# Turning q and k of a transformer's second layer by VectorE blocks and GpSimd copies instead of TensorE transposes

## The chip, the cores and the metric

The kernel runs on one core of a Trainium2 chip. The metric is the device time of one execution in microseconds. A core has five engines that run side by side, each with its own queue of instructions worked off in order: TensorE (PE in the profile; the loads of its weights are PEld), VectorE (DVE), ScalarE (ACT), GpSimd (POOL) and SyncE (SP), which issues the DMAs here. Engines wait for each other by semaphores.

## The reference

An encoder of two layers on 256 tokens of 2048 features, all in float32. Each layer has a mixer sub-layer and a gated MLP. What matters here is the mixer's beginning:

```python
h = rmsnorm(x, norm_mix[l]) * (1.0 + sc_a) + sh_a
qa, ka, va, qb, kb, vb, ga, gb = split_cols(h @ w_in[l])
qa = rotary_partial(rmsnorm(qa.reshape(B, S, HA, HEAD_DIM), qn_a[l]), pos)
ka = rotary_partial(rmsnorm(ka.reshape(B, S, GA, HEAD_DIM), kn_a[l]), pos)
ya = window_attention(qa, ka, va, sink_a[l]) @ w_proj_a[l]
qb = rmsnorm(qb.reshape(B, S, HB, HEAD_DIM), qn_b[l])
kb = rmsnorm(kb.reshape(B, S, HB, HEAD_DIM), kn_b[l])
yb = neighbourhood_attention(qb, kb, vb, rel_bias_b[l]) @ w_proj_b[l]
merged = jax.nn.sigmoid(ga) * ya + jax.nn.sigmoid(gb) * yb
```

Mixer A has 8 query heads on 2 key heads, mixer B 8 heads; a head has 128 features. q and k are normalised for each head and token, scaled by a gain per feature, and in mixer A rotated in the first 32 features. Both attentions are softmaxes over the 256 tokens with a mask (A, with a sink logit) or a bias (B).

## The kernel before, in words

The weights (units of 128 x 2048 numbers, `ws`) come from HBM one after the other in the order of their use. Each unit is split into two halves by `unit_steps`: ScalarE casts a half to a rounded part (L319), VectorE subtracts it from the weights to get the rest (L320), both into a tile `hl` with four buffers. TensorE multiplies with three matmuls for each product (rounded by rounded, rounded by rest, rest by rounded: L336 to L338 in `feature_block`, L399 to L401 in `tokens`).

The projection to q, k and v is done in nine groups of 512 columns, group 0 to 8. Group 0 holds the keys and values of mixer A, 1 and 2 its queries (four heads each); 3, 4, 5 hold keys, values and queries of mixer B's first four heads, 6, 7, 8 those of the others. A group is four units long. `tokens` leaves a group with the 256 tokens on partitions, in two PSUM tiles `ps_t` of 128 tokens. The attention wants q and k with the features on partitions, so each group but the values' is turned in `qk_rows`:

- at once: squares summed per head by ScalarE (L569), roots by VectorE and GpSimd (`rsqrt`, L462 and L463);
- `norm`: VectorE multiplies by the roots into `qn` (L578), a tile with one buffer, and in groups 0 to 2 rotates (L593 to L595);
- `turn`: TensorE transposes each head's 128x128 block of `qn` into PSUM (L602), and ScalarE scales by the gain into the pack of the mixer (L603). Then the group counts as ready.

The background work hangs on `bg`, whose `tick` runs at the end of each unit. `defer` puts a function at the next tick: `norm` runs three ticks after the group, `turn` four. A job such as `attention` is stepped at a rate, a number of steps per tick. In each step of `attention` every living head goes one stage on, and one more head starts if the group that it waits for is ready. The stages of a head (`head_a`, `head_b`, `attend`) are: splitting of q and k; scores and softmax; turning of the probabilities; their split and the split of v; the product with v (`po`). In the second layer the probabilities are already turned without TensorE, by `turned_blocks`: VectorE transposes all 32x32 blocks (L293), and GpSimd puts the blocks in their places with 16 copies (L298).

The functions only trace instructions. The order on each engine is made afterwards by a planner (Tile's scheduler), which takes from the instructions that it expects to be ready the one that was traced first. So an instruction traced late can stand early in its engine's queue.

In the second layer the stretch runs thus: 8 units of mixer A's gate, the nine groups (36 units), the remaining gate (8), the projection of mixer A (8), mixer B's gate (16). All A heads must be done before the projection of mixer A, all B heads before that of mixer B.

## Time and profile before

| what | value |
|---|---|
| median of 3 runs | 2657.92 us (2656.72 to 2659.6) |
| profiled execution | 2660.64 us, its span 2658.7 us |
| TensorE busy | 2646.4 us of the span |
| VectorE busy | 2116.5 us |
| ScalarE busy | 1407.9 us |
| GpSimd busy | 194.0 us |
| GpSimd's copies L298 in the second layer | 256, from 1511.0 to 1748.6 us |
| transposes L602 of q and k | 104, 52 of them in the second layer |

Rows of the profile name a line of the kernel, an engine, an operation, the tile written and those read, and the shapes (partitions x elements). A row of the timeline begins with its start in the span and its duration; in square brackets stands how long the engine had been idle before it, and what ended that. In a row of groups, the numbers behind the bar are busy us, mean ns of one, and the idle time before. A row for a tile or a line gives the shortest, the median and the longest duration in ns, and the first and the last start. "PE sc L629 <- ACT packB L603" in the waits is a wait of TensorE, at the instruction that writes `sc`, for ScalarE's that writes `packB`; total us, times and the longest follow. A cast or a matmul's record can overlap the next one on its engine.

### The profile page before, as it was taken

Reading aid. Unit: us, or ns where it says so; the run is one execution under the profiler, and the core shown is the slowest. Engines: PE = TensorE matmul, PEld = TensorE weight load, DVE = VectorE, ACT = ScalarE, POOL = GpSimd, SP = SyncE. Lnnn points to the kernel's source line nnn. Section 1 sums busy time; section 2 is a strip of 40 time slices with the busy share of each in tenths; the row PEclk is TensorE's granted clock in tenths of the full one; section 3 lists DMA queues with packets and bytes.
Section 4 is the critical chain, followed back from the end, with each engine's and each line's share of the span. In section 5 each row is a group of like instructions: output and inputs, shape, how many; then the busy total and the mean of one; then the engine's idle time right before and its main releaser. Section 6 shows DMA issues by size and latency. Waiting matters only on the chain.

```text
span 2658.7 us, 51010 instructions
## 1 busy us (share of the span) xinstructions
PE 2646.4 (100%) x21192; PEld 2561.3 (96%) x21192; DVE 2116.5 (80%) x2975; ACT 1407.9 (53%) x2284; POOL 194.0 (7%) x281
## 2 busy tenths in 40 slices
PE   9999999999999999999999999999999999999999
PEld 7888899999999999999998889999999999999999
DVE  8898998897987888788886677868888866655664
ACT  5445865456653555355554566645565445544553
POOL 0001100000000000000000177610000000000000
PEclk9999999999999999999999999999999999999999
DMA  9988779885778788877856666766747775555554
GB/s 359 350 329 300 257 296 353 319 327 193 283 294 297 282 293 296 297 288 285 296 213 255 237 236 235 255 256 260 279 180 286 295 254 191 191 197 193 196 190 143
DMA packets 102042, 700.43 MB, mean 263 GB/s; under 512 B 12721, under 2 KB 15025, under 8 KB 17969
## 3 DMA queue, kind: packets, MB, share of 16 engines
q1 hardware_dynamic: 101810, 697.17, 71.3%
q8 instruction: 166, 2.72, 0.4%
q14 instruction: 66, 0.54, 0.1%
HBM read 695.03 MB, written 2.10 MB: 262 GB/s over the span
## 4 chain that ended last, share of the span: by engine, by line
PE 88%; DVE 5%; POOL 2%; ACT 2%; DMA 1%; issue 1%; DVEq 0%; ACTq 0%; POOLq 0%
PE ps L336 26%; PE ps L338 26%; PE ps L337 26%; PE ps_t L401 3%; PE ps_t L400 3%; PE ps_t L399 3%; POOL p L298 2%; DVE hl L320 2%; DMA aw<-in_aw 1%; DVE aw L230 1%; ACT hl L319 1%; PE sc L629 1%; PE po L667 1%; POOL qrs L463 0%; ACT qsq L569 0%
## 5 line engine op out<-in xcount | busy, mean ns | idle before, releaser
L320 DVE TENSOR_TENSOR hl<-w,hl 128x1024 fp32r<-128x1024 f32 x928 | 1129.8, 1224 | 308.6 <-ACT hl L319 304.6
L319 ACT CAST hl<-w 128x1024 fp32r<-128x1024 f32 x928 | 969.7, 1048 | 704.7 <-PE ps L338 494.0
L336 PE MATMUL ps<-h,hl 128*128 128x256 f32 x3328 | 922.5, 277 | 1.3 <-DVE ya L948 0.6
L337 PE MATMUL ps<-h,hl 128*128 128x256 f32 x3328 | 919.7, 276 | 0.0
L338 PE MATMUL ps<-h,hl 128*128 128x256 f32 x3328 | 919.6, 277 | 0.0
L336 PEld LDWEIGHTS ps<-h,hl 128*128 128x128 f32 x3328 | 624.8, 188 | 2.3 <-DVE ya L948 0.8
L337 PEld LDWEIGHTS ps<-h,hl 128*128 128x128 f32 x3328 | 625.2, 188 | 0.4 <-DVE h L492 0.2
L338 PEld LDWEIGHTS ps<-h,hl 128*128 128x128 f32 x3328 | 624.3, 188 | 0.0
L230 DVE CUSTOM_DVE_ANT_0 aw<-aw,cact,ab 128x2048 f32<-128x2048 f32 x189 | 443.8, 2349 | 73.8 <-DMA aw<-in_aw 73.4
L399 PE MATMUL ps_t<-hl,h 128*128 128x512 f32 x576 | 223.4, 393 | 2.1 <-ACT h L491 1.6
L400 PE MATMUL ps_t<-hl,h 128*128 128x512 f32 x576 | 224.9, 391 | 0.4
L401 PE MATMUL ps_t<-hl,h 128*128 128x512 f32 x576 | 224.3, 390 | 0.0
L1027 DVE SCALAR_TENSOR_TENSOR u<-ps,cw,u 128x255 f32<-128x255 f32 x304 | 146.1, 481 | 63.0 <-ACT u L1025 58.9
L1025 ACT ACTIVATE u<-ps,cw 128x256 f32<-128x256 f32 x152 | 85.7, 564 | 157.0 <-PE ps L338 156.9
L336 PE MATMUL ps<-merged,hl 128*128 128x256 f32 x512 | 141.8, 278 | 0.8 <-DVE m L425 0.8
L338 PE MATMUL ps<-merged,hl 128*128 128x256 f32 x512 | 141.7, 277 | 0.0
L337 PE MATMUL ps<-merged,hl 128*128 128x256 f32 x512 | 141.7, 277 | 0.0
L337 PE MATMUL ps<-act_o,hl 128*128 128x256 f32 x512 | 141.4, 276 | 0.0
L338 PE MATMUL ps<-act_o,hl 128*128 128x256 f32 x512 | 141.4, 276 | 0.0
L336 PE MATMUL ps<-act_o,hl 128*128 128x256 f32 x512 | 141.2, 276 | 0.0
L399 PEld LDWEIGHTS ps_t<-hl,h 128*128 128x128 f32 x576 | 107.9, 188 | 25.4 <-ACT h L491 2.6
L400 PEld LDWEIGHTS ps_t<-hl,h 128*128 128x128 f32 x576 | 108.1, 188 | 24.0 <-DVE hl L320 2.1
(239 smaller groups left out, 4774.5 us busy)
## 6 DMA issues: line engine op xcount, KB each, us to landing
w<-in_ws SPq DMA_DIRECT2D x463, 1024.0 KB, 4.9
aw<-in_aw SPq DMA_DIRECT2D x189, 1024.0 KB, 6.1
p<-in_bias SPq DMA_DIRECT2D x16, 256.0 KB, 4.5
x<-in_xT SPq DMA_DIRECT2D x4, 512.0 KB, 5.4
aw_o<-in_aw SPq DMA_DIRECT2D x2, 1024.0 KB, 12.5
out<-x SPq DMA_DIRECT2D x16, 128.0 KB, 2.2
w<-in_ws SPq DMA_DIRECT2D x2, 512.0 KB, 11.8
aw_b<-in_aw SPq DMA_DIRECT2D x1, 1024.0 KB, 17.1
```

Of the source, the lines that this page charges most:

```text
L230: nc.vector.tensor_tensor_reduce(out=raw[:], in0=raw[:], in1=cact[:], scale=1.0, scalar=ab[:, i : i + 1], op0=ALU.mult, op1=ALU.add, accum ...
L298: nc.gpsimd.tensor_copy(out=dst[a : a + BLOCK, :, :, b : b + BLOCK], in_=blocks[b : b + BLOCK, :, :, a : a + BLOCK])
L319: nc.scalar.copy(hl[:, 0], r)
L320: nc.vector.tensor_tensor(out=hl[:, 1], in0=r, in1=hl[:, 0].bitcast(F32), op=ALU.subtract)
L336: nc.tensor.matmul(out, hi, act[0], start=first, stop=False)
L337: nc.tensor.matmul(ps[:, :S], hi, act[1], start=False, stop=False)
L338: nc.tensor.matmul(out, lo, act[0], start=False, stop=last)
L399: nc.tensor.matmul(ps[:], xh, hi, start=kc == kcs[0], stop=False)
L400: nc.tensor.matmul(ps[:], xh, lo, start=False, stop=False)
L401: nc.tensor.matmul(ps[:], xl, hi, start=False, stop=kc == kcs[-1])
L1025: nc.scalar.activation(out=u, in_=ps, func=AF.Identity, scale=w[:, 1:2], bias=w[:, 3:4])
L1027: nc.vector.scalar_tensor_tensor(out=u[:, to], in0=ps[:, of], scalar=w[:, j : j + 1], in1=u[:, to], op0=ALU.mult, op1=ALU.add)
```

## The change

In the second layer, groups 0, 1, 2 and 8 are no longer transposed by TensorE. VectorE transposes the 32x32 blocks of `qn` in place, GpSimd puts them into the pack with 16 copies (of 32 partitions and 128 elements in group 0, 256 in the others), and three ticks later ScalarE scales the pack in place by the gain; then the group is ready. `qn` is laid out without holes for that. The first layer and groups 3, 5 and 6 keep the transposes.

In the second layer the `attention` job is added after group 1 instead of group 2, at 0.4 steps a tick instead of 0.43. The first four A heads wait for groups 0 and 1, the other four for group 2; before, all waited for group 2.

```diff
-ATT = [1.288, 0.43]
+ATT = [1.288, 0.4]
+EARLY = {1: 2}
+MOVED_QK = [(), (0,1,2,8)]
+QK_STEPS = 3
...
+    def moved_blocks(dst, src):
+
+        for b in range(0, P, BLOCK):
+            for a in range(0, P, BLOCK):
+                nc.gpsimd.tensor_copy(
+                    out=dst[a : a + BLOCK, :, :, b : b + BLOCK], in_=src[b : b + BLOCK, :, :, a : a + BLOCK]
+                )
+
...
-            qn = at.tile([P, 2, 4, HEAD], F32, name="qn", tag="qn", bufs=1)
+            qn = at.tile([P, 8 * HEAD], F32, name="qn", tag="qn", bufs=1)[:, : 2 * n]
+            qn = qn.rearrange("p (t h d) -> p t h d", t=2, d=HEAD)
...
         def turn(qn):
+            if moved:
+                nc.vector.transpose(out=qn, in_=qn)
+                moved_blocks(dst.rearrange("p h (t s) -> p h t s", t=2), qn.rearrange("p t h d -> p h t d"))
+
+                def scaled():
+                    nc.scalar.activation(out=dst, in_=dst, func=AF.Identity, scale=gain)
+                    then()
+
+                later(QK_STEPS, scaled)
+                return
...
-            todo = [(3, head_a, i) for i in range(HA)] + [(6 + 3 * (i // 4), head_b, i) for i in range(HB)]
+            todo = [(EARLY[l] + i // 4, head_a, i) if l in EARLY else (3, head_a, i) for i in range(HA)] + [(6 + 3 * (i // 4), head_b, i) for i in range(HB)]
...
-                if g == 2:
+                if g == (1 if l in EARLY else 2):
                     bg.add(job, ATT[l])
```

The calls of `qk_rows` pass `g in MOVED_QK[l]` as `moved`; `turned_blocks` calls `moved_blocks` for its copies.

More of the change, by code (lines that the diff above doesn't have):

```diff
@@ L295, in turned_blocks @@
         dst = src.rearrange("p t (n k) -> p (t n k)", n=n).rearrange("p (n t k) -> p n t k", n=n, t=2)
-        for b in range(0, P, BLOCK):
-            for a in range(0, P, BLOCK):
-                nc.gpsimd.tensor_copy(
-                    out=dst[a : a + BLOCK, :, :, b : b + BLOCK], in_=blocks[b : b + BLOCK, :, :, a : a + BLOCK]
-                )
+        moved_blocks(dst, blocks)
     def unit_steps(l, u, by_halves=False):
@@ L559, in level, with qk_rows @@
             return z, sh
-    def qk_rows(pss, heads, rot, gain, dst, then):
+    def qk_rows(pss, heads, rot, gain, dst, then, moved=False):
         cols = 0
@@ L575, in norm @@
         def norm():
-            qn = at.tile([P, 2, 4, HEAD], F32, name="qn", tag="qn", bufs=1)
+            qn = at.tile([P, 8 * HEAD], F32, name="qn", tag="qn", bufs=1)[:, : 2 * n]
+            qn = qn.rearrange("p (t h d) -> p t h d", t=2, d=HEAD)
             for t, ps in enumerate(pss):
                 nc.vector.tensor_tensor(
-                    out=qn[:, t, :heads],
+                    out=qn[:, t],
                     in0=ps[:, cols : cols + n].rearrange("p (h d) -> p h d", d=HEAD),
@@ L584, in norm @@
             if rot is not None:
-                x1, x2 = qn[:, :, :heads, :HALF], qn[:, :, :heads, HALF:ROT]
+                x1, x2 = qn[:, :, :, :HALF], qn[:, :, :, HALF:ROT]
                 tab = [rot[:, i].unsqueeze(2).broadcast_to([P, 2, heads, HALF]) for i in range(4)]
@@ L930, in encoder @@
                 if g == 0:
-                    qk_rows(pss, GA, rots[1], gains[:, 1:2], kTa, turned)
+                    qk_rows(pss, GA, rots[1], gains[:, 1:2], kTa, turned, g in MOVED_QK[l])
                 elif g < 3:
-                    qk_rows(pss, 4, rots[0], gains[:, 0:1], dst, turned)
+                    qk_rows(pss, 4, rots[0], gains[:, 0:1], dst, turned, g in MOVED_QK[l])
                 elif vcol is None:
-                    qk_rows(pss, 4, None, gains[:, 3:4] if g in (3, 6) else gains[:, 2:3], dst, turned)
+                    qk_rows(pss, 4, None, gains[:, 3:4] if g in (3, 6) else gains[:, 2:3], dst, turned, g in MOVED_QK[l])
                 else:
                     turned()
-                if g == 2:
+                if g == (1 if l in EARLY else 2):
                     bg.add(job, ATT[l])
```

## Prediction

> **What bounds the kernel now.** First the page's busy line and its chain of waits, then the stretches of the second layer that the change touches, then the waits of PE in them.

> ```profile
> span 2658.7 us, 51010 instructions
> ...
> PE 2646.4 (100%) x21192; PEld 2561.3 (96%) x21192; DVE 2116.5 (80%) x2975; ACT 1407.9 (53%) x2284; POOL 194.0 (7%) x281
> ...
> PE 88%; DVE 5%; POOL 2%; ACT 2%; DMA 1%; issue 1%; DVEq 0%; ACTq 0%; POOLq 0%
> ```

> ```profile
> core 0: us, PE busy (x) PEld busy (x) DVE busy (x) ACT busy (x) POOL busy (x), PEclk, DMA share, GB/s
> 1421.00:1510.00 89.00, 89.00 (x406) 73.83 (x406) 60.31 (x86) 48.75 (x101) 6.00 (x4) 1.00 0.66 242
> 1510.00:1602.00 92.00, 92.00 (x447) 77.43 (x446) 69.49 (x115) 58.92 (x132) 61.38 (x100) 1.00 0.61 225
> 1602.00:1669.00 67.00, 66.56 (x560) 65.45 (x559) 54.25 (x89) 44.17 (x95) 44.01 (x68) 1.00 0.70 252
> ```

> ```profile
> PE sc L629 <- ACT packB L603: 0.4, 1, 0.4
> ```

> TensorE is the bound: busy for all but 12.3 us of a span of 2658.7, at clock 1.00, and over the whole stretch from 1377 to 1850 us it waited once, for 0.4 us (last fence), for the evacuation of group 8's transposes. VectorE has a fifth to a third of these stretches free, ScalarE a third to a half. GpSimd does almost nothing until 1510, and then works two thirds of the time on the heads' copies. So the change can gain only what it takes off TensorE, and can lose only by making TensorE wait. It waits when the split weights (hl) come late, since ScalarE (L319) and VectorE (L320) make them in order behind everything else that stands in their queues.

> **What is removed from TensorE.** Groups 1, 2 and 8 lose 8 transposes each, group 0 (two heads) 4: 28 of the second layer's 52. The record of one lasts 0.272 us, but PE's records overlap; what counts is from start to start.

> ```profile
> L602 PE MATMUL qtp<-ident,qn 128*128 128x128 f32 x52 | 6.8, 272 | 0.0
> ```

> ```profile
> 1463.53 0.39 PE L400 MATMUL ps_t<-hl,h 128*128 128x512 f32 x1
> 1463.76 0.39 PE L401 MATMUL ps_t<-hl,h 128*128 128x512 f32 x1
> 1463.99 1.03 PE L602 MATMUL qtp<-ident,qn 128*128 128x128 f32 x8
> 1464.78 0.48 PE L399 MATMUL ps_t<-hl,h 128*128 128x512 f32 x1
> 1465.09 0.39 PE L400 MATMUL ps_t<-hl,h 128*128 128x512 f32 x1
> ```

> ```profile
> 1441.71 0.60 PE L602 MATMUL qtp<-ident,qn 128*128 128x128 f32 x4
> 1442.07 0.48 PE L399 MATMUL ps_t<-hl,h 128*128 128x512 f32 x1
> 1442.38 0.39 PE L400 MATMUL ps_t<-hl,h 128*128 128x512 f32 x1
> ```

> Matmuls of 512 columns start 0.23 us apart. From the first transpose of eight to the second matmul behind them it is 1465.09 - 1463.99 = 1.10 us; less the 0.23 of the matmul between, eight cost 0.87 us. Four cost 1442.38 - 1441.71 - 0.23 = 0.44. Together 3 x 0.87 + 0.44 = 3.05 us, and with the 0.4 us wait of sc for group 8's evacuation, which goes too, **3.5 us**. The excess of start distances elsewhere in the stretch does not hang on the transposes.

> [...]

> **What is added beside TensorE.** The rows that price it: a block transpose, an evacuation, a cast of 1024 elements.

> ```profile
> L293 DVE STREAM_TRANSPOSE packB<-p x8: 700/712/712, 1633.2 to 1738.6; 128x512 f32<-128x512 f32 x8
> ```

> ```profile
> L603 ACT ACTIVATE packB<-qtp,gains 128x512 f32<-128x512 f32 x8 | 5.0, 682 | 0.5 <-PE qtp L602 0.5
> ```

> ```profile
> L319 ACT CAST hl<-w 128x1024 fp32r<-128x1024 f32 x928 | 969.7, 1048 | 704.7 <-PE ps L338 494.0
> ```

> VectorE: one block transpose for each group, in place. A 128x512 one takes 0.71 us, so 0.71 for group 0 and between 0.71 and 1.42 for each of the others; I take 1.4, 4.9 us in all. They fit in the free time of the stretches above (28.7 of 89 us, 12.8 of 67). ScalarE: two evacuations of 0.68 us become one instruction over 1024 elements, priced by the hl cast of that size, 1.05: a small gain off the path, priced at nothing. The changed layout of qn and the reads of the rotary on it have the same counts and sizes: nothing.

> ```profile
> L298 POOL COPY p<-spare x16: 285/290/2316, 1511.0 to 1518.9; 32x128 f32<-32x128 f32 x16
> ```

> ```profile
> masks.py:197 POOL MEMSET ident<- 128x128 f32 x1 | 0.2, 205 | 0.3 <-POOLq L1174 0.3
> ...
> L1174 POOL MEMSET const-float32-0.0<- 128x1 f32 x1 | 0.1, 99 | 0.2 <-issue 0.2
> ```

> GpSimd: 64 copies. Group 0's are 32x128, like the 256 of the heads; the others have 32x256, which no row shows. Below they can't be under the 0.285 us of 32x128, above not over twice that, 0.57. Nearest are the fills: 127 more elements cost 205 - 99 = 106 ns. So I take 0.39, or 1.6 us more for 16 copies.

> **The wait that is added.** The scaling on ScalarE now follows 16 copies. QK_STEPS sets it three ticks later in the program (a tick is a unit of weights, 24 of the matmuls above, 5.5 us). But that is only its priority. The norm of group 8 stands three ticks, 16 us, behind its squares and roots, and ran right behind the roots:

> ```profile
> 1614.36 1.64 POOL L463 TENSOR_TENSOR qrs<-qss,mhalf 128x8 f32<-128x8 f32 x1 [1.72 <-DVE qss L462]
> ```

> ```profile
> 1616.03 0.69 DVE L578 TENSOR_TENSOR qn<-ps_t,qrs 128x512 f32<-128x512 f32 x1 [1.81 <-POOL qrs L463]
> ```

> So an instruction is queued where the planned order has its inputs ready. Queued behind it on ScalarE are the hl casts, and behind those VectorE's subtractions and TensorE. The trace shows this very wait once, at head 0 of mixer A:

> ```profile
> 1511.04 8.18 POOL L298 COPY p<-spare 32x128 f32<-32x128 f32 x16 [15.99 <-DVE spare L293]
> ```

> ```profile
> 1512.38 1.06 ACT L319 CAST hl<-w 128x1024 fp32r<-128x1024 f32 x1
> 1519.25 0.62 ACT L411 CAST pT<-p 128x512 fp32r<-128x512 f32 x1 [5.80 <-POOL p L298]
> 1519.77 3.89 ACT L319 CAST hl<-w 128x1024 fp32r<-128x1024 f32 x4
> ```

> ```profile
> 1512.17 2.35 DVE L230 CUSTOM_DVE_ANT_0 aw<-aw,cact,ab 128x2048 f32<-128x2048 f32 x1 [1.26 <-DMA aw<-in_aw]
> ...
> 1520.85 1.23 DVE L320 TENSOR_TENSOR hl<-w,hl 128x1024 fp32r<-128x1024 f32 x1 [5.10 <-ACT hl L319]
> ```

> ```profile
> 1522.64 0.40 PE L399 MATMUL ps_t<-hl,h 128*128 128x512 f32 x1
> ```

> Sixteen copies took 8.18 us; ScalarE came to its cast 2.4 us after they began (1519.25 - 5.80 - 1511.04) and stood 5.8 us. The half unit cast behind it was ready at 1520.85 + 1.23 = 1522.08, and TensorE took it up at 1522.64 without idling: 0.6 us were left. So a wait of ScalarE for GpSimd is free up to about **6.4 us**, and costs TensorE one for one beyond.

> The copies' time holds waits of their own: the longest of these sixteen lasted 2.316 us, beside the 2.35 us of L230. [...]

> How far sixteen copies of a head stretch:

> ```profile
> 1620.41 12.36 POOL L298 COPY p<-packA 32x128 f32<-32x128 f32 x16 [4.41 <-DVE packA L293]
> 1633.96 7.71 POOL L298 COPY p<-packB 32x128 f32<-32x128 f32 x16 [1.18 <-DVE packB L293]
> 1645.41 12.63 POOL L298 COPY p<-packB 32x128 f32<-32x128 f32 x16 [3.74 <-issue]
> ```

> *Group 0*: the case of head 0, 5.8 us, nothing lost. If its copies stretch to 12.63, as in the last row, the wait is 10.2 and 3.8 are lost.

> *Groups 1 and 2*: 8.18 + 1.6 = 9.8 us of copies. ScalarE comes to the scaling 2.4 us behind their begin if the order expects no more of the larger copies, and at 2.4 x 9.8 / 8.18 = 2.9, or up to 3.1 by the bare copies, if it does. I take 3.1: a wait of 6.7, 0.3 lost by each. Ends: nothing (copies as short as 32x128), and with 0.57 us each 12.6 of copies, a wait of 10.2 and 3.8 lost by each.

> *Group 8* comes when GpSimd is occupied (the first two rows of the last fence):

> ```profile
> 1617.84 0.69 DVE L578 TENSOR_TENSOR qn<-ps_t,qrs 128x512 f32<-128x512 f32 x1
> 1619.64 0.71 DVE L293 STREAM_TRANSPOSE packA<-p 128x512 f32<-128x512 f32 x1
> ```

> ```profile
> 1634.71 0.64 ACT L411 CAST pT<-p 128x512 fp32r<-128x512 f32 x1
> ```

> Its qn is normed at 1618.5, just ahead of the last A head's transpose (1619.64), whose copies now fill 1620.4 to 1632.8. Whichever set comes second ends 9.8 us later, near 1642.6. With group 8 first, its scaling loses 0.3, and the head's cast, which ScalarE reached at 1634.71, waits 7.9 and loses 1.5: 1.8. I take this order, as qn is ready first. The low end is nothing; the high end is below.

> The earlier start of A's heads and the rate of 0.4 move little: by the ticks, head 0 starts one tick earlier, heads 4 to 7 at the same ticks as now, B's heads a tick later, and the job ends three ticks ahead of the end of gate B instead of four, so that nothing is run off in a lump. Cost nothing; if it ended late, the remaining heads' chains would lie bare on TensorE.

> **The sum.** -3.5 + 0 + 0.3 + 0.3 + 1.8 = -1.1 us. The profiled execution took 2660.64 us (1.9 outside its span), 2.7 above the median of the runs, 2657.92; taken off the median: **2656.8 us**.

> **The rivals.** What a measurement of this kernel can tell from no change is about 0.2%, 5.3 us.

> *Slower: group 8 stands behind the A head's copies.* Then its scaling is due about 3 us after qn, near 1623, and GpSimd is done with it at 1642.6: a wait of 19 us, 13 lost: -3.5 + 0.6 + 13, or 2668. It decides from a wait of some 15 us on. For it: GpSimd is busy two thirds of that stretch. Against it: qn is ready first. [...] Chance 0.25.

> *Slower: 32x256 copies cost double.* Groups 1, 2 and 8 lose 3.8 each and the A head 4.5: -3.5 + 15.9, or 2670. For it: nothing shows that a copy's time has a fixed part. Against it: the fills, 128 times the elements in 2.1 times the time. Chance 0.12.

> *All hidden.* The planned order allows enough, no wait passes 6.4 us: 2654.4. For it: VectorE is lighter before 1510 than at head 0. Against it: head 0, where the order came to its wait after 2.4 of 8.18 us. Chance 0.15.

> *A transpose is worth its whole record.* 28 x 0.272 = 7.6 us: 2650.3, the only way to faster by over 5.3. Against it: the starts, 0.11 apart. Chance 0.06.

> The forecast itself, the saving mostly kept or mostly handed back (2654 to 2663): 0.42. So faster 0.07, same 0.56 and slower 0.37. The range leaves out the doubled copies' upper half and the whole record: 2653 to 2670.

> **What would show it.** In the second layer 24 rows of qtp instead of 52, and the other starts on PE no further apart. New L298-like copies into packA and packB, 64, at 0.39 us where undisturbed. ScalarE rows of the scaling with gaps on GpSimd near 6 us for groups 0 to 2; PE idle before hl's users next to them if the gap passes 6.4. It is wrong if these gaps are missing (planned order slower than I think), or if PE idles by more than 5 us around 1620 to 1650.

## The result and the profile after

The changed kernel takes 2681.83 us, median of five runs (2679.93 to 2682.58), beside 2657.06 us for the kernel before (five runs, 2656.57 to 2659.6): a ratio of 1.0089, interval 1.0078 to 1.0101. It is 24.8 us slower, and the prediction had it at 2656.8 us, in a range up to 2670. The profiled execution took 2680.73 us.

The busy line of the changed kernel's page, and TensorE's waits from 1377 to 1850 us (total us, times, longest):

```profile
span 2679.0 us, 51014 instructions
...
PE 2649.3 (99%) x21164; PEld 2560.7 (96%) x21164; DVE 2121.0 (79%) x2979; ACT 1411.6 (53%) x2280; POOL 214.1 (8%) x345
```

```profile
PE ps_t L406 <- ACT hl L326: 8.0, 3, 5.1
PE ps L343 <- ACT hl L326: 5.9, 1, 5.9
PE ps_t L407 <- DVE hl L327: 2.0, 3, 0.8
PE sc L647 <- ACT packB L621: 1.9, 1, 1.9
PE ps L345 <- DVE hl L327: 0.5, 1, 0.5
```

Line numbers have moved: the cast into hl is L326 (was L319), the subtraction L327, the matmuls L406 to L408 and L343 to L345; L608 is the new transpose in place, L612 the new scaling. Where TensorE waited once for 0.4 us, it now waits 18.3 us, all but 1.9 of it for hl. And it is busy for 2.9 us more, though it runs 28 instructions fewer. The same windows as the prediction showed of the kernel before say why: the granted clock (PEclk) is no longer 1.00.

```profile
core 0: us, PE busy (x) PEld busy (x) DVE busy (x) ACT busy (x) POOL busy (x), PEclk, DMA share, GB/s
1421.00:1510.00 89.00, 78.99 (x329) 63.34 (x328) 56.40 (x77) 39.29 (x82) 32.38 (x52) 0.94 0.57 212
1510.00:1602.00 92.00, 90.00 (x431) 74.99 (x430) 66.85 (x108) 58.31 (x128) 42.53 (x86) 1.00 0.61 226
1602.00:1669.00 67.00, 60.60 (x435) 57.29 (x434) 45.91 (x74) 36.55 (x79) 46.04 (x78) 0.95 0.57 207
```

What holds hl up is ScalarE. Its timeline around the four scalings (start, duration, instruction, and in brackets the idle time before it and what ended that):

```profile
1425.02 1.05 ACT L326 CAST hl<-w 128x1024 fp32r<-128x1024 f32 x1 [1.67 <-PE ps_t L408]
1433.85 0.72 ACT L612 ACTIVATE packA<-packA,gains 128x512 f32<-128x512 f32 x1 [7.78 <-POOL packA L298]
...
1453.77 1.05 ACT L326 CAST hl<-w 128x1024 fp32r<-128x1024 f32 x1 [1.67 <-PE ps_t L408]
1465.32 1.15 ACT L612 ACTIVATE packA<-packA,gains 128x1024 f32<-128x1024 f32 x1 [10.49 <-POOL packA L298]
1466.37 1.03 ACT L326 CAST hl<-w 128x1024 fp32r<-128x1024 f32 x1
...
1492.36 1.15 ACT L612 ACTIVATE packA<-packA,gains 128x1024 f32<-128x1024 f32 x1 [12.75 <-POOL packA L298]
...
1648.15 1.15 ACT L612 ACTIVATE packB<-packB,gains 128x1024 f32<-128x1024 f32 x1 [13.31 <-POOL packB L298]
1649.21 1.03 ACT L326 CAST hl<-w 128x1024 fp32r<-128x1024 f32 x1
```

GpSimd's timeline gives the copies that it waits for:

```profile
1424.90 8.92 POOL L298 COPY packA<-qn 32x128 f32<-32x128 f32 x16 [3.75 <-DVE qn L608]
...
1456.54 8.74 POOL L298 COPY packA<-qn 32x256 f32<-32x256 f32 x16 [6.15 <-DVE qn L608]
...
1481.62 10.70 POOL L298 COPY packA<-qn 32x256 f32<-32x256 f32 x16 [6.15 <-DVE qn L608]
...
1630.47 9.33 POOL L298 COPY packB<-qn 32x256 f32<-32x256 f32 x9 [3.94 <-DVE qn L608]
1639.84 5.22 POOL L298 COPY p<-packA 32x128 f32<-32x128 f32 x16
1645.11 3.01 POOL L298 COPY packB<-qn 32x256 f32<-32x256 f32 x7
```

ScalarE came to the scaling at 1433.85 - 7.78 = 1426.1 us, 1.2 us after group 0's copies had begun. In group 1 it came at 1454.8, in group 2 at 1479.6: 1.7 and 2.0 us *before* the copies began. In group 1 VectorE had not even begun its transpose, as its timeline shows; its next subtraction then stood 8.5 us for ScalarE's cast:

```profile
1455.24 1.24 DVE L608 STREAM_TRANSPOSE qn<-qn 128x1024 f32<-128x1024 f32 x1
...
1467.43 1.23 DVE L327 TENSOR_TENSOR hl<-w,hl 128x1024 fp32r<-128x1024 f32 x1 [8.51 <-ACT hl L326]
```

In group 8 GpSimd put a head's 16 copies between nine and seven of the group's. So ScalarE stood 7.8, 10.5, 12.8 and 13.3 us.

After the stall of group 2, TensorE's timeline reads:

```profile
1494.49 0.80 PE L406 MATMUL ps_t<-hl,h 128*128 128x512 f32 x1 [5.09 <-ACT hl L326]
1495.75 0.79 PE L407 MATMUL ps_t<-hl,h 128*128 128x512 f32 x1 [0.47 <-DVE hl L327]
1496.35 0.63 PE L408 MATMUL ps_t<-hl,h 128*128 128x512 f32 x1
1496.77 0.63 PE L406 MATMUL ps_t<-hl,h 128*128 128x512 f32 x1
...
1499.60 0.39 PE L407 MATMUL ps_t<-hl,h 128*128 128x512 f32 x1
1499.83 0.39 PE L408 MATMUL ps_t<-hl,h 128*128 128x512 f32 x1
```

The matmuls start 0.43 us apart until 1499.3, then 0.23 again: half speed. The trace's records of the clock show half speed for 3.41 us from 1468.7, for 6.83 from 1492.6 and for 6.83 from 1649.6; the windows' 0.94 over 89 us and 0.95 over 67 come to the same (twice 0.06 x 89 + 0.05 x 67 is 17.4 us at half).

What each stall costs, start to start (from the last matmul before it to the first at full spacing after it, less the usual spacing of 0.23 us, or 0.113 for 256 columns, for each start between):

| group | ScalarE's wait | beyond 6.4 us | TensorE lost | more than one for one |
|---|---|---|---|---|
| 0 | 7.8 | 1.4 | 1.5 | 0.1 |
| 1 | 10.5 | 4.1 | 5.6 | 1.5 |
| 2 | 12.8 | 6.4 | 8.1 | 1.7 |
| 8 | 13.3 | 6.9 | 9.5 | 2.6 |
| sum | | 18.8 | 24.7 | 5.9 |

With the 1.9 us wait of sc, and less the 3.5 us of the transposes, that is +23.1. Measured over the stretch it is +23.5: I counted TensorE's instructions from the program's start to the first behind 1380 us of the trace before, and from its end to the first behind 1850 us; between these two lie 470.1 us before and 493.6 after. (The untouched part ahead varies by up to 4.5 us from one profiled execution to another, and the profiled one of before was long there, so that the spans differ by 20.3 only.) "The stretch" below is always this one.

### The profile page after: what moved, and what is told of

It is laid out like the page before. It is cut to its first block, busy times and chain, and to the rows that moved or that the text cites. A ratio compares the mean times of both kernels' runs of the same rounds, so it can differ in the third digit from the quotient of the medians.

```text
span 2679.0 us, 51014 instructions
## 1 busy us (share of the span) xinstructions
PE 2649.3 (99%) x21164; PEld 2560.7 (96%) x21164; DVE 2121.0 (79%) x2979; ACT 1411.6 (53%) x2280; POOL 214.1 (8%) x345
## 5 line engine op out<-in xcount | busy, mean ns | idle before, releaser
L327 DVE TENSOR_TENSOR hl<-w,hl 128x1024 fp32r<-128x1024 f32 x928 | 1130.3, 1225 | 320.9 <-ACT hl L326 318.1
L326 ACT CAST hl<-w 128x1024 fp32r<-128x1024 f32 x928 | 970.2, 1049 | 708.5 <-PE ps L345 506.5
L343 PE MATMUL ps<-h,hl 128*128 128x256 f32 x3328 | 923.9, 278 | 7.2 <-ACT hl L326 6.1
L345 PE MATMUL ps<-h,hl 128*128 128x256 f32 x3328 | 920.9, 277 | 0.5 <-DVE hl L327 0.5
L343 PEld LDWEIGHTS ps<-h,hl 128*128 128x128 f32 x3328 | 626.0, 188 | 8.5 <-ACT hl L326 6.8
L345 PEld LDWEIGHTS ps<-h,hl 128*128 128x128 f32 x3328 | 625.5, 188 | 0.8 <-DVE hl L327 0.8
L406 PE MATMUL ps_t<-hl,h 128*128 128x512 f32 x576 | 224.7, 395 | 10.1 <-ACT hl L326 8.5
L408 PE MATMUL ps_t<-hl,h 128*128 128x512 f32 x576 | 225.6, 393 | 0.0
L406 PEld LDWEIGHTS ps_t<-hl,h 128*128 128x128 f32 x576 | 108.9, 189 | 35.2 <-ACT hl L326 10.2
L345 PE MATMUL ps<-merged,hl 128*128 128x256 f32 x512 | 141.5, 277 | 0.0
L343 PE MATMUL ps<-merged,hl 128*128 128x256 f32 x512 | 141.5, 277 | 0.0
L345 PE MATMUL ps<-act_o,hl 128*128 128x256 f32 x512 | 141.3, 276 | 0.0
L343 PE MATMUL ps<-act_o,hl 128*128 128x256 f32 x512 | 141.2, 276 | 0.0
## 6 DMA issues: line engine op xcount, KB each, us to landing
aw_o<-in_aw SPq DMA_DIRECT2D x2, 1024.0 KB, 12.6
```

Of the source, the lines that this page charges most:

```text
L326: nc.scalar.copy(hl[:, 0], r)
L327: nc.vector.tensor_tensor(out=hl[:, 1], in0=r, in1=hl[:, 0].bitcast(F32), op=ALU.subtract)
L343: nc.tensor.matmul(out, hi, act[0], start=first, stop=False)
L345: nc.tensor.matmul(out, lo, act[0], start=False, stop=last)
L406: nc.tensor.matmul(ps[:], xh, hi, start=kc == kcs[0], stop=False)
L408: nc.tensor.matmul(ps[:], xl, hi, start=False, stop=kc == kcs[-1])
```

## The experiments

Three explanations were open. *The order*: ScalarE reaches the scaling before its copies are done, because the planner queued it there. *The added work*: 64 copies and four transposes slow VectorE's subtractions, whoever waits for them. *The heads*: the earlier start and the rate of A's heads bring the loss. Each time below has the ratio to the kernel before of the same comparison, with its interval.

**The scaling behind the casts.** The scaling must be issued after the weight cast that was traced last; nothing else is changed.

```diff
-            nc.scalar.copy(hl[:, 0], r)
+            last_cast[0] = nc.scalar.copy(hl[:, 0], r).ins
...
-                    nc.scalar.activation(out=dst, in_=dst, func=AF.Identity, scale=gain)
+                    with tc.issue_after(last_cast[0]):
+                        nc.scalar.activation(out=dst, in_=dst, func=AF.Identity, scale=gain)
```

> The changed kernel with one difference: each scaling of a turned group is queued on ScalarE behind the last weight cast that is traced by then (5 to 7 casts later than in the changed kernel, 14 to 19 us); transposes, copies, their order on VectorE and GpSimd and the heads' schedule stay. Theory Q (ScalarE stands at a scaling that is queued too early, and the weight casts behind it make TensorE wait): no wait of ScalarE for GpSimd at the scalings, the 25 us vanish and the removed transposes show: 2653 to 2656 us (before 2657.1, changed 2681.8). Rival C (the added blocks and copies hold up VectorE and GpSimd themselves): stays at 2675 or more. Rival S (the heads' earlier start and slower rate): stays at 2675 or more.

It took 2658.26 us, 1.0004 (0.9996 to 1.0013): 23.6 us of the 24.8 are gone. TensorE's waits in the stretch, then ScalarE's and GpSimd's timelines at group 1:

```profile
PE sc L649 <- ACT packB L623: 2.5, 1, 2.5
PE ps_t L408 <- DVE hl L328: 0.8, 1, 0.8
```

```profile
1465.76 1.05 ACT L327 CAST hl<-w 128x1024 fp32r<-128x1024 f32 x1 [1.26 <-PE ps_t L409]
1466.72 1.15 ACT L614 ACTIVATE packA<-packA,gains 128x1024 f32<-128x1024 f32 x1
```

```profile
1452.57 13.48 POOL L299 COPY packA<-qn 32x256 f32<-32x256 f32 x16 [6.35 <-DVE qn L609]
```

ScalarE now comes to the scaling at 1466.7, after the copies' end at 1466.05, and idles for none of groups 0 to 2. The copies take longer than in the changed kernel, 13.5 us against 8.7: there VectorE stood still from 1458.9 to 1467.4 us beside them, here its longest wait for a cast, from 1400 to 1800 us, is 2.3 us. It does no harm. The order is the cause of nearly all of the loss.

**Many more ticks.** If ticks set the place, eight instead of three should cure it.

```diff
-QK_STEPS = 3
+QK_STEPS = 8
```

> The changed kernel with eight ticks instead of three between the copies and the scaling. Theory Q: the number sets only the place in the program, ScalarE's queue has the scalings at the same casts, the waits of 8 to 13 us stay: 2677 to 2688 us. If three ticks were too short a time for the copies: 2660 or less.

2691.91 us, 1.0132 (1.0116 to 1.0147), above all that was expected. ScalarE's waits:

```profile
ACT packA L612 <- POOL packA L298: 30.4, 3, 12.9
...
ACT packB L612 <- POOL packB L298: 13.4, 1, 13.4
```

In the changed kernel they are 31.0 in total for groups 0 to 2 (7.78 + 10.49 + 12.75) and 13.3. Five ticks more, 27 us, moved nothing: the number of ticks is a priority and no place. What is longer here are the heads, which come later; it was not followed further.

**The added work without the wait.** Groups 0, 1 and 2 are transposed by TensorE as before. Beside it VectorE transposes the blocks and GpSimd makes the 48 copies, into a part of a pack that nobody uses; so this kernel does work for nothing. Group 8 is as before the change, the heads as after it.

```diff
-MOVED_QK = [(), (0,1,2,8)]
+MOVED_QK = [(), (0,1,2)]
...
-                nc.vector.transpose(out=qn, in_=qn)
-                moved_blocks(dst.rearrange("p h (t s) -> p h t s", t=2), qn.rearrange("p t h d -> p h t d"))
...
+                work = scr[0][:, :8].rearrange("p c s -> p (c s)")
+                blocks = work[:, : 2 * n].rearrange("p (t h d) -> p t h d", t=2, d=HEAD)
+                put = work[:, 8 * HEAD : 8 * HEAD + 2 * n]
+                nc.vector.transpose(out=blocks, in_=qn)
+                moved_blocks(put.rearrange("p (h t s) -> p h t s", t=2, s=HEAD), blocks.rearrange("p t h d -> p h t d"))
```

> Groups 0, 1 and 2 are transposed by TensorE and scaled as before; beside it VectorE's block transposes and GpSimd's 48 copies run too, into an unused part of a pack, and nothing waits for them. The heads' schedule is that of the change. Theory Q: the added work alone costs little, 2656 to 2661 us. Rival C: the same stalls as the changed kernel has for these groups, some 14 us: 2668 to 2674.

**The heads alone.** The earlier start and the rate of 0.4, with all groups transposed by TensorE.

```diff
-MOVED_QK = [(), (0,1,2,8)]
+MOVED_QK = [(), ()]
```

> Only the heads' schedule of the change (start after group 1, heads waiting for their own group, rate 0.4); all groups are transposed by TensorE as before. Theory Q and rival C: 2656 to 2660 us, the schedule costs nothing. Rival S: most of the 25 us, 2670 to 2682.

The two belong together: 2664.35 us, 1.0029 (1.0017 to 1.0042), with the added work, and 2663.8, 1.0027 (1.0017 to 1.0036), without it. The windows of the two, the one with the work first:

```profile
1400.00:1510.00 110.00, 107.35 (x489) 88.75 (x488) 77.27 (x108) 59.47 (x124) 51.59 (x71) 1.00 0.63 234
```

```profile
1400.00:1510.00 110.00, 107.75 (x491) 89.13 (x490) 72.23 (x105) 58.55 (x123) 12.04 (x22) 1.00 0.62 234
```

In these 110 us GpSimd is busy for 39.6 us more and VectorE for 5.0 more, TensorE for 0.4 less; the medians are 0.55 us apart. The added work costs next to nothing as long as nobody waits for it. But the heads alone cost 6.8 us, which the prediction had at nothing. TensorE's waits with the heads alone:

```profile
PE ps_t L407 <- DVE hl L327: 2.7, 2, 2.2
PE sc L647 <- ACT packB L621: 2.5, 1, 2.5
PE ps L345 <- DVE hl L327: 0.2, 1, 0.2
```

The wait of 2.5 us, followed back through the timelines of GpSimd, VectorE, ScalarE and TensorE:

```profile
1539.82 6.12 POOL L298 COPY p<-packA 32x128 f32<-32x128 f32 x16 [3.05 <-DVE amod L240]
1546.02 1.64 POOL L470 TENSOR_TENSOR qrs<-qss,mhalf 128x8 f32<-128x8 f32 x1
```

```profile
1547.69 1.29 DVE L586 TENSOR_TENSOR qn<-ps_t,qrs 128x512 f32<-128x512 f32 x2 [6.00 <-POOL qrs L470]
```

```profile
1557.50 0.51 ACT L658 ACTIVATE p<-p,nm 128x256 f32<-128x256 f32 x1 [5.18 <-DVE nm L655]
```

```profile
1563.70 0.97 PE L647 MATMUL sc<-kA,qA 128*128 128x256 f32 x6 [2.49 <-ACT packB L621]
```

A group's roots (L470) stand behind a head's copies in GpSimd's queue. VectorE stands 6.0 us for them in order, then ScalarE 5.2 for VectorE, and at last TensorE 2.5 for an evacuation. The 2.2 us come by way of head 0's cast, as the next but one experiment shows.

**Turning alone.** The heads and their rate as before the change; all four groups turned the new way.

```diff
-ATT = [1.288, 0.4]
-EARLY = {1: 2}
+ATT = [1.288, 0.43]
+EARLY = {}
```

> Only the turning of groups 0, 1, 2 and 8 of the change; the heads start and run as before (after group 2, rate 0.43). Theory Q and rival C: 2677 to 2685 us, as the change. Rival S: 2654 to 2660.

2685.77 us, 1.0105 (1.0091 to 1.0119), with ScalarE's waits of 29.8 us for groups 0 to 2 and 14.6 for group 8. The parts do not add up: turning alone costs 28.8 us, the heads alone 6.8, both together 24.8. Turning alone was 23.9 us at half clock (records of 6.83, 6.83 and 10.24), both together 17.1; by an estimate from that, half of the 6.8 us between them, 3.4, explains a part. That one cause also hides in the stalls of the other is likely, but not shown.

**Heads' copies behind the roots.** As the heads alone; in addition a head's copies must be issued after the roots traced last.

```diff
-        nc.gpsimd.tensor_tensor(out=dst, in0=src, in1=mhalf[:, :k], op=ALU.pow)
+        last_pow[0] = nc.gpsimd.tensor_tensor(out=dst, in0=src, in1=mhalf[:, :k], op=ALU.pow).ins
...
-        moved_blocks(dst, blocks)
+        with tc.issue_after(last_pow[0]):
+            moved_blocks(dst, blocks)
```

> The heads' schedule of the change alone (2663.8 us), with one difference: the copies of a head may not be queued on GpSimd ahead of the roots of a group that was traced before them, so that group 5's roots stand ahead of 16 copies instead of behind them. Theory P (VectorE stands 6.0 us at group 5's norm for roots queued behind copies, ScalarE's softmax and casts behind it, and TensorE's scores behind those): the 2.5 us wait of the scores goes, and 1 us beside it: 2659 to 2661 us; the 2.4 us at head 0's cast stay. If the schedule costs by itself: 2663 to 2665.

2661.07 us, 1.0013 (1.0004 to 1.0022): 2.7 us less than the heads alone. One wait of TensorE is left in the stretch, and beside it one of ScalarE, 6.7 us for GpSimd at head 0's cast of the probabilities:

```profile
PE ps_t L409 <- DVE hl L329: 2.2, 1, 2.2
...
ACT pT L420 <- POOL p L299: 6.7, 1, 6.7
```

The stretch takes 472.2 us, 2.1 more than before: the whole of that wait. (Of ScalarE's 6.7 us 4.5 were free here, not 6.4.) The medians are 4.1 us apart, with an interval from 1.1 to 5.8, and the profiled execution, 2659.08 us, was 2.0 faster than its median; so the 2.1 fit, and the rest can't be told from the spread.

**Everything, with three orders fixed.** The whole change, with the scaling behind the casts, the heads' copies behind the roots, and the split of the probabilities behind the casts too.

```diff
-        split(pT, tp[:])
+        with (tc.issue_after(last_cast[0]) if rows is not None else nullcontext()):
+            split(pT, tp[:])
```

> The changed kernel with its heads' schedule and all four groups, and three orders set: scalings queued behind the casts of three ticks later, roots ahead of later heads' copies, and the heads' casts pT behind the weight casts traced before them. Theories Q and P together: no wait left, 28 transposes and the 0.4 us wait gone, 2653 to 2655 us (before 2657.0; 2658.3 with the scalings alone set behind). If the added work costs by itself: 2657 or more.

2654.6 us, 0.9992 (0.9983 to 1.0000). TensorE waits nowhere in the stretch, which takes 466.4 us, 3.7 less than before. The prediction's worth of the transposes and of the wait that goes with them was 3.5.

**Three or two groups, the heads as before.** The scaling behind the casts, rate and start of the heads as before the change, groups 0, 1 and 8.

```diff
-MOVED_QK = [(), (0,1,2,8)]
+MOVED_QK = [(), (0,1,8)]
```

> As the last, and group 8 too: 20 transposes go, 2.2 us, and with them the 0.4 us wait of the scores for group 8's evacuation. Theory Q: 2653.5 to 2656 us. Rival: group 8's copies among those of the heads make a head's cast late and TensorE wait: 2658 to 2663.

The same with groups 0 and 1 only:

```diff
-MOVED_QK = [(), (0,1,2,8)]
+MOVED_QK = [(), (0,1)]
```

> Groups 0 and 1 alone turned by VectorE and GpSimd, their scalings queued behind the casts of three ticks later; the heads start and run as in the kernel before. 12 of the 28 transposes go: 0.44 + 0.87 = 1.3 us. Theory Q with the schedule's own cost (6.8 us, heads' schedule alone): no wait at the scalings, 2655 to 2657 us (before 2657.0). Rival C: 3 us or more slower than before.

Three groups: 2654.25 us, 0.9989 (0.9981 to 0.9998), below the kernel before by more than the interval, and the lowest median of all (the 2654.6 above can't be told from it). Two groups: 2655.46, 0.9993 (0.9984 to 1.0002). The stretch is shorter by 2.9 us for 20 transposes and the wait of sc, and by 1.3 for 12 transposes, 0.11 us each. With three groups TensorE waits nowhere in the stretch, although ScalarE still stood 3.1 us for group 8.

**All four, heads as before, one tick.** The order is fixed as above, but the scaling is traced one tick behind the copies instead of three, so that it stands closer behind them.

```diff
-ATT = [1.288, 0.4]
-EARLY = {1: 2}
+ATT = [1.288, 0.43]
+EARLY = {}
...
-QK_STEPS = 3
+QK_STEPS = 1
```

> All four groups, heads as in the kernel before, scalings queued behind the casts of one tick later: 3, 1, 2 and 2 casts later than in the changed kernel, 2.7 us each. By theory Q the waits of ScalarE there shrink from 7.8, 10.5, 12.8 and 13.3 us to about 0, 8, 7 and 8; each beyond 6 costs one for one and the clock stays full: -3.5 + 5 = +1.5, 2656 to 2661 us. Rival C: 2670 or more, since all added work is there.

2671.34 us, 1.0058 (1.0044 to 1.0072), more than expected. ScalarE's waits:

```profile
ACT packA L614 <- POOL packA L299: 20.4, 3, 9.6
...
ACT packB L614 <- POOL packB L299: 11.3, 1, 11.3
```

With the edge, then, ticks do count: it binds the scaling to a cast of the tick in which it was traced, and the copies of groups 1 and 2, 11.6 and 12.5 us here, need more than one tick of 5.5. ScalarE's waits of 9.6 and 11.3 us were followed by half clock on TensorE again (3.41 us from 1494.1 and from 1644.2). Ahead of a third record, from 1657.9, stands another wait: ScalarE's of 6.2 us for VectorE, at a head's softmax.

**Group 8 alone.** The changed kernel, with only group 8 turned the new way.

```diff
-MOVED_QK = [(), (0,1,2,8)]
+MOVED_QK = [(), (8,)]
```

> The changed kernel, group 8 alone turned by VectorE and GpSimd, heads' schedule as changed (2663.8 us by itself). Theory Q: one wait of ScalarE of 12 to 14 us, TensorE idle some 6 us and at half clock for 3 to 7 us behind it: 2670 to 2674 us. If the groups' waits act on each other: under 2667.

2670.65 us, 1.0052 (1.0039 to 1.0066), as expected, but not in the way expected: without groups 0 to 2 the group's copies were not split by a head's (16 in one row, from 1623.25 to 1631.94), and ScalarE stood only 5.7 us.

```profile
ACT packB L612 <- POOL packB L298: 5.7, 1, 5.7
```

It still cost 6.9 us over the heads alone. Some 1.6 us of that arise long before group 8: head 0's wait of 2.2 us, which both kernels have, is followed here by 3.41 us at half clock (from 1504.7), and with the heads alone it is not. The last section sets the two beside each other. At group 8 TensorE waited 1.9 and 3.6 us for hl, although ScalarE stood for less than 6.4, and 6.83 us at half clock begin at 1637.8. TensorE had not waited for over 50 us before, so hl was not late already. But 3.5 us of other work, the scaling included, stood on ScalarE between the wait and the next weight cast (1631.97 to 1635.49), and VectorE, which had stood 7.4 us for ScalarE's softmax, came to its next subtraction only at 1639.3. So the 6.4 us of head 0 do not hold where, as here, that much stands between the wait and the next weight cast and subtraction.

**Six groups.** Groups 3, 5 and 6 as well, with the scaling behind the casts, the heads as before.

```diff
-MOVED_QK = [(), (0,1,2,8)]
+MOVED_QK = [(), (0,1,3,5,6,8)]
```

> Groups 0, 1, 3, 5, 6 and 8 turned by VectorE and GpSimd, scalings behind the casts of three ticks later, heads as in the kernel before: 44 transposes go, 0.44 + 5 x 0.87 = 4.8 us, and the 0.4 us. Theory Q alone: 2652 to 2653 us. Theory P: groups 3, 5 and 6 put their copies among the heads' and the roots, VectorE and ScalarE stand for them, 2656 to 2666.

2664.8 us, 1.0032 (1.0019 to 1.0044). What waits now is VectorE, at the norm, for roots that stand behind copies on GpSimd:

```profile
DVE qn L587 <- POOL qrs L471: 21.3, 7, 9.6
```

TensorE then waits 9.5 us for hl in all, and runs at half clock for 6.83 us. While the heads' copies fill GpSimd, this gain can't be had without an order for the roots too; that version was not tried.

## Why the prediction was wrong

*The worth of the transposes* was right. Start to start they were put at 0.109 us each and 3.5 us with the wait of sc; the stretch gives 3.7 less where nothing waits, and 0.11 each for groups 0 and 1. The record's 0.27 us, and the rival built on it (2650.3), are refuted. The two runs of 2654 us, which have the queue orders set and 28 and 20 of these transposes fewer on TensorE, are 2.4 and 2.7 us below the kernel before of their comparisons.

*The prices of the added work* were right. The rows of the changed kernel for the copies, the transposes in place, and the transposes left on TensorE (the second: shortest, median and longest in ns, first and last start):

```profile
L298 POOL COPY packB<-qn x16: 390/398/2362, 1630.5 to 1647.7; 32x256 f32<-32x256 f32 x16
```

```profile
L608 DVE STREAM_TRANSPOSE qn<-qn x4: 712/1240/1245, 1424.0 to 1629.1; 128x1024 f32<-128x1024 f32 x3, 128x512 f32<-128x512 f32 x1
```

```profile
L620 PE MATMUL qtp<-ident,qn 128*128 128x128 f32 x76 | 10.6, 274 | 0.0
```

A copy of 32x256 lasts 0.39 to 0.40 us (predicted 0.39), so the rival of doubled copies falls, although its time, 2670, was nearer. A transpose of 128x1024 lasts 1.24 us (predicted 1.4). And 76 transposes are left, 52 in the first layer and 24 in the second, as said. That this work is hidden on VectorE and GpSimd held as well: 48 copies and three transposes moved the median by 0.55 us, less than the intervals can tell.

*The mechanism* was right: ScalarE stands in order at the scaling, the casts of hl behind it are late, and TensorE waits from about 6.4 us on. Group 0 shows that bound best: 7.8 us of wait, 1.5 lost, so 6.3 free. But it is no constant. At head 0 of the run with the roots in order 4.5 were free, and at group 8 alone hardly any of 5.7 (TensorE waited 5.5): what stands in the queues between the wait and the next weight cast and subtraction counts too. It was also right that the ticks are only a priority.

Four steps failed.

1. *"ScalarE comes to the scaling 2.4 us behind their begin ... or up to 3.1 by the bare copies ... I take 3.1."* Measured: 1.2 us after the begin in group 0, 1.7 and 2.0 us before it in groups 1 and 2. The only row like it was head 0's, with one transpose ahead of the copies. Groups 1 and 2 have the roots, the norm, the rotary and the transpose ahead of them, 6.15 us from the roots' end to the copies in each (GpSimd's idle time in its row), and the order had the scaling too early for all of that. By how much the planner misjudges each link is in no trace and stays open. The waits were 7.8, 10.5 and 12.8 us instead of 5.8, 6.7 and 6.7.
2. *Group 8: "Whichever set comes second ends 9.8 us later."* Neither came second. Nine of its copies ran, then the head's 16, then the other seven, and ScalarE came 4.4 us after the first of them. The wait was 13.3 us, not 6.7; the head's cast did not wait there. The rival that had it behind the head came nearer, with a wait of 19 us and 13 lost; measured are 13.3 and 9.5, by another order. Both steps together are worth 18.8 - 2.4 = 16.4 us, at one for one.
3. *"Costs TensorE one for one beyond."* Stalls of 3.5 to 6.4 us were followed by half clock, 5.9 us more in the table above. TensorE's busy time says the same: 2.9 us up, where the transposes take 3.05 out. The length of a stall alone does not give this term: the same 2.2 us were followed by half clock in one run and not in another (last section).
4. *"The earlier start of A's heads and the rate of 0.4 ... Cost nothing."* Alone they cost 6.8 us; beside the other stalls only the 1.9 us wait of sc is left of it. The step looked at when the heads start, not at what their copies push back in GpSimd's queue: a group's roots. It also had head 0 one tick (5.5 us) earlier. With the heads alone its copies began at 1495.9 us instead of 1511.0, so 15.1 earlier; 2.3 of these lie ahead of the stretch.

16.4 + 5.9 + 1.9 = 24.2 us, beside 24.6 between the predicted -1.1 and the measured +23.5. In the prediction's own words it was to be wrong "if PE idles by more than 5 us around 1620 to 1650": it idled 6.4.

## What to carry to other kernels

An instruction that waits for a slow engine must be looked at for what stands behind it in its own queue: if that is the feed of the engine that bounds the kernel, the length of the wait counts, and a start "some ticks later" in the program is no place in the queue, while an explicit order behind the feed's last instruction is. To forecast such a wait, don't take over the arrival seen at another place; add up every link between the inputs and the wait, since each that runs later than planned lengthens it, and then what stands between the wait and the feed's next instruction. And a saving of 3.5 us on the bounding engine is lost with the first stall that is 4 us too long (group 1's wait, 4.1 us beyond 6.4, cost 5.6).

## What the runs showed of the hardware

In the changed kernel TensorE's stalls of 3.5, 5.6 and 6.4 us (groups 1, 2 and 8) cost more than their own length: 5.6, 8.1 and 9.5 us. After waits of 0.9 us (group 0) the clock stayed whole; 2.8 and 0.8 us close together (group 1) were followed by 3.41 us at half clock, 5.1 and 0.5 (group 2) and 5.9 and 0.5 (group 8) by records of 6.83, of which a part fell into the stall itself. The starts of 512-column matmuls went from 0.23 to 0.43 us apart.

So a stall of the same length cost more in one run than in another. Head 0's 2.2 us fell into a single step with group 8 alone (1501.3 to 1504.7), and the half clock behind it cost 1.6 us. With the heads alone they fell across two steps, 1.41 and 0.84, and the clock stayed whole.

GpSimd's copies took longer where VectorE worked beside them. Sixteen of 32x256 (group 1) took 8.7 us where VectorE stood still for most of them, and 13.5 in the run where it did not, while the median of the sixteen is 0.40 us in both: two copies of 1.30 us make the difference in the one, six of 1.29 to 2.36 in the other. What 48 such copies, 16 of them 32x128, cost TensorE when nobody waited for them is too little to tell: the medians are 0.55 us apart.
